# One square for both sums of a norm, and the second layer's memory products moved into latent attention

## The chip, the core and the metric

The kernel runs on one core of a Trainium2 chip. The metric is the device time of one execution in microseconds. All times below are of that core. "PE" is TensorE, "DVE" VectorE, "ACT" ScalarE, "POOL" GpSimd, "SP" the engine that issues most transfers; "PEld" is TensorE's load of the stationary operand, which overlaps its products.

## The reference

Two blocks run one after the other on a sequence of 512 rows of 1024 numbers. The first block ends in a mixture of experts and a norm with factor `final_norm_g`. The second block has two layers; each begins with a norm, so that at the seam two norms follow each other directly. Each layer computes three attentions (sliding window, sparse, latent), joins them, and then attends to a memory of 256 rows:

```python
def rmsnorm(x, g):
    x32 = x.astype(jnp.float32)
    y = x32 * lax.rsqrt(jnp.mean(x32 * x32, axis=-1, keepdims=True) + NORM_EPS)
    return (y * g.astype(jnp.float32)).astype(x.dtype)

for l in range(DEPTH_2):
    h = rmsnorm(x, norm_mix[l])
    ...                      # w_in, window, sparse and latent attention, w_out
    x = x + cross_attn(rmsnorm(x, norm_xattn[l]), rmsnorm(mem, norm_mem[l]),
                       w_xq[l], w_xkv[l], w_xo[l])
    ...                      # feed-forward
```

In `cross_attn` the memory side is `hm @ w_kv`, a 256 x 1024 by 1024 x 1024 product: columns 0 to 511 are the keys of four heads, 512 to 1023 their values. It depends on the inputs alone, not on x, so each layer's can be computed at any time before that layer's cross attention.

## The kernel before

Activations of block 2 lie transposed: eight tiles of 128 partitions (channels) by 512 columns (rows of the sequence), `xT[:, k]`. Most products are made in float32r with both operands split into a high and a low part (`hi_lo`, L36): three products for each chunk of 128 channels (`mmT`, L1173, lines L1179 to L1181), summed in a PSUM bank. `block128` (L1183) loads 128 columns of a weight, splits them (ACT high, DVE low) and makes the 24 products of eight chunks into a bank with tag "mm", of which there are two. Weights pass through three raw tiles (`wr`) and two split ones each (`wh`, `wl`).

The order of the work: the kernel is written as straight code, and a planner orders each engine's instructions by a simulated time, with earlier program text first. `self.fill` is a list of pieces of work; `pump` (L1000) takes some from it, and `share` (L1008) spreads the rest over the heads that are left, so that PE has something to do while a head's softmax runs on ACT and DVE.

`first_norm` (L1126) is the seam between the blocks. `norm_add` makes the high and low parts of x times both factors (`nh`, `nl`). For the sums it makes two squares for each chunk, of x (ACT and POOL in turn, L1139 and L1141) and of x times `final_norm_g` (ACT, L1142), and sums each over its 128 channels with a float32 product against 32 columns of ones (L1144), four chunks side by side in the four 32-row quarters of one bank, so two banks. Both are copied (L1146, L1147); eight float32 products with the column `pick` (L1151) add the four quarters and turn the sums into columns; a dozen small DVE steps make the two inverse roots, and `spread` (L132, product on L135, copy on L136) makes rows of them. The products of layer 0 don't wait for these rows: `scaled` (L1189) applies r to a bank behind the products. `layer` (L1382) begins with columns 512 (keys) and 640 (values) of `w_in_2` for the sliding window.

`mem_kv` (L1743) makes layer 1's memory products in eight parts of 128 columns behind a `start` that loads the normed memory `mh` (two halves, high and low, written to DRAM by `memory`, L1086, during block 1). Each part loads weights, splits them (L1760 on ACT, L1761 on POOL or DVE), makes 24 products of 256 columns, splits the result and stores it (L1774). Parts 4 to 7 also turn the result with two transposes (L1772). Parts 0 to 3 are put in at the end of `first_norm` (L1167), parts 4 to 7 before layer 0's cross attention (L1535), which takes them as fill (L1781, L1838). Layer 0's own memory products (`mem_kv0`, L1720) are made in block 1 in plain float32. The latent attention is the loop `self.heads(mla, oc)` (L1522) with the list of L1521 as fill.

Of the kernel before, what the change touches and what calls it, by code (L numbers as in the profile page):

```python
# [24 lines left out]
class Kern:  # L25
# [158 lines left out]
    def run(self):  # L184
        tc, nc, a = self.tc, self.nc, self.a
        with tc.tile_pool(name="cst", bufs=1, reuse_waits="tile") as self.cst, tc.tile_pool(name="dr0", bufs=1, space=bass.MemoryType.DRAM) as self.dram0, ExitStack() as self.late:
            cst = self.cst
            self.pst = "t"
            self.nraw, self.nw = 0, 0
            self.fill, self.side, self.kvd = [], [], [self.dram0.tile([8, P, 512], F32, name=f"kv{l}") for l in range(2)]  # L190
            self.xT = cst.tile([P, ND, T], F32, name="xT")
            self.ident = self.const("k_ident")
            self.ones = cst.tile([P, P], F32, name="ones")
            nc.vector.memset(self.ones, 1.0)
            self.pick = cst.tile([P, 1], F32, name="pick")
            nc.vector.reduce_sum(self.pick, self.ident[:, 0:P:32], axis=AX)
            self.block1()
            self.block2()
# [773 lines left out]
    def unit(self, name, dt=F32R):  # L972
        return self.sp.tile([P, 512], dt, tag="un", name=name, bufs=self.NU)
# [4 lines left out]
    def block2(self):  # L978
# [92 lines left out]
    def memory_rows(self):  # L1071

        nc = self.nc
        self.memd = self.dram0.tile([P, 2, 4, 512], F32, name="memd")
# [11 lines left out]
    def memory(self, tms, i):  # L1086
# [6 lines left out]
        m = [self.tmp("m", F32R) for _ in range(2)]  # L1093
        for s in range(2):
# [31 lines left out]
    def first_norm(self):  # L1126
# [22 lines left out]
        for i in range(2):  # L1149
            for t in range(NT):  # L1150
                nc.tensor.matmul(ps[:, 4 * i + t:4 * i + t + 1], rows[i][:, t * P:(t + 1) * P], self.pick, start=True, stop=True)  # L1151
        v = self.sp.tile([P, 8], F32, name="v8")
        nc.vector.tensor_scalar(v, ps[:, :8], 1.0 / D, None, op0=ALU.mult)
# [13 lines left out]
        self.fill += self.mem_kv(1, range(4), True)  # L1167
        self.pump(4)
# [213 lines left out]
    def layer(self, l, h, r, xd):  # L1382
# [7 lines left out]
        va = self.v_stack(self.scaled(self.block128(W, 640, h), r))  # L1390
# [130 lines left out]
        self.fill += [lambda: pair(1)] + b1[0:1] + [lambda: pair(2)] + b1[1:2] + [lambda: pair(3)] + b1[2:]  # L1521
# [12 lines left out]
        if l == 0:  # L1534
            self.fill += self.mem_kv(1, range(4, 8))  # L1535
# [207 lines left out]
    def mem_kv(self, l, parts, pool=False):  # L1743

        nc, a = self.nc, self.a
        W = a["w_xkv_2"][l]
        hm = ([], [])
        d = self.kvd[l]

        def start():  # L1750
            for i in range(4):
                for z in range(2):
                    m = self.unit("mh")
                    nc.sync.dma_start(m.bitcast(F32), self.memd[:, z, i])
                    hm[z].extend(m[:, 256 * s:256 * s + 256] for s in range(2))

        def part(i):
            raw = self.wraw(W, 0, ND, i * P, P)
            w = self.wtiles(ND, P)
            nc.scalar.copy(w[0], raw)  # L1760
# [4 lines left out]
            if i < 4:  # L1765
                self.hi_lo(ps[:, :256], t[:, 0:256], t[:, 256:512])
            else:
                f = self.tmp("xv")
                nc.scalar.copy(f[:, :256], ps[:, :256])
                pt = self.bank("pt", 2)  # L1770
                for q in range(2):
                    nc.tensor.transpose(pt[:, q * P:(q + 1) * P], f[:, q * P:(q + 1) * P], self.ident)  # L1772
                self.hi_lo(pt[:, :256], t[:, 0:256], t[:, 256:512])
            nc.sync.dma_start(d[i], t.bitcast(F32))  # L1774
# [212 lines left out]
```

## Time and profile before

| | |
|---|---|
| median of three runs | 3110.28 us (3108.94 to 3110.70) |
| profiled execution | 3112.91 us, its span 3111.1 us |
| PE busy | 2962.9 us (95%) |
| DVE, ACT, POOL busy | 1805.3, 1295.6, 170.6 us |
| mean granted TensorE clock | 0.983 |
| mean load of the DMA engines | 159 GB/s |

The span runs from the first to the last instruction; the execution has 1.8 us around it. The page cuts the span into 40 slices: PE is at 9 tenths or more in nearly all. Block 1 and the experts take the first 1006 us, layer 0 the time to about 2070, layer 1 the rest. Matmuls are pipelined, so their durations overlap; the step from one start to the next is what a product costs.

### The profile page before, as it was taken

The page shows a single profiled execution, that of the slowest core. Times are in us where ns is not written, and L with a number is a line of the kernel's source. Part 1 is how long each engine was busy: PE and PEld are TensorE (multiplying, and loading weights), DVE is VectorE, ACT ScalarE, POOL GpSimd, SP SyncE. Part 2 cuts the span into 40 slices and gives each one's busy share as a digit, 9 for nine tenths or more (in the row PEclk, how much of TensorE's full clock was granted, in tenths as well). Part 3 has the DMA queues.
Part 4 walks back from the last instruction along what each step waited for, and adds up shares of the span by engine and source line. Part 5 has one row for each costly group of instructions (what it writes and reads, how often), then busy time and mean ns, then how long its engine had stood idle before and what let it go on. Part 6 is the DMA issues. An engine that isn't in the chain of part 4 may idle for free.

```text
span 3111.1 us, 39214 instructions
## 1 busy us (share of the span) xinstructions
PE 2962.9 (95%) x14752; PEld 2237.4 (72%) x14752; DVE 1805.3 (58%) x3246; ACT 1295.6 (42%) x2482; POOL 170.6 (5%) x163
## 2 busy tenths in 40 slices
PE   7999999998987999999999999999999999999998
PEld 2887776443322788887878888878888887788886
DVE  7566774343334666567666553556766777655354
ACT  5333342322222444468645322233555775432233
POOL 1000211000000100000110000000000002000000
PEclk8998999999999999999999999999999999999999
DMA  7433677999999542223253333344322234233332
GB/s 256 123 99 101 195 228 276 384 409 409 409 409 367 147 114 73 73 85 104 79 167 111 102 89 101 90 118 115 89 70 78 83 93 132 91 109 90 102 94 81
DMA packets 478113, 493.57 MB, mean 159 GB/s; under 512 B 30182, under 2 KB 381668, under 8 KB 477924
## 3 DMA queue, kind: packets, MB, share of 16 engines
q1 hardware_dynamic: 474260, 481.05, 47.1%
q0 software_dynamic: 2224, 5.82, 0.6%
q10 hardware_dynamic: 1440, 4.19, 0.4%
q8 instruction: 116, 1.90, 0.3%
q14 instruction: 73, 0.60, 0.1%
HBM read 458.76 MB, written 32.24 MB: 158 GB/s over the span
## 4 chain that ended last, share of the span: by engine, by line
PE 59%; DVE 4%; ACT 3%; issue 1%; POOL 0%; ACTq 0%; DVEq 0%; POOLq 0%
PE mm L1179 11%; PE mm L1180 11%; PE mm L1181 11%; PE s L1181 3%; PE s L1180 3%; PE s L1179 3%; PE o L1179 3%; PE o L1180 3%; PE o L1181 3%; PE s L1274 2%; PE pt L1258 1%; PE o L1300 1%; DVE wl L40 1%; ACT p L1284 1%; ACT p L1277 1%
## 5 line engine op out<-in xcount | busy, mean ns | idle before, releaser
L39 ACT CAST wh<-wr 128x1024 fp32r<-128x1024 f32 (+6 forms) x433 | 377.1, 874 | 827.7 <-issue 264.6
L40 DVE TENSOR_TENSOR wl<-wr,wh 128x1024 fp32r<-128x1024 f32 (+7 forms) x431 | 459.2, 1068 | 232.1 <-ACT wh L39 230.2
L1179 PE MATMUL mm<-nh,wh 128*128 128x512 f32 x1136 | 449.7, 396 | 9.4 <-DVE gt L1541 4.4
L1181 PE MATMUL mm<-nh,wl 128*128 128x512 f32 x1136 | 447.3, 394 | 0.1
L1180 PE MATMUL mm<-nl,wh 128*128 128x512 f32 x1136 | 446.1, 393 | 0.0
L1179 PEld LDWEIGHTS mm<-nh,wh 128*128 128x128 f32 x1136 | 214.2, 189 | 56.2 <-DVE gt L1541 7.3
L1181 PEld LDWEIGHTS mm<-nh,wl 128*128 128x128 f32 x1136 | 214.3, 189 | 44.4 <-issue 0.8
L1180 PEld LDWEIGHTS mm<-nl,wh 128*128 128x128 f32 x1136 | 214.2, 189 | 43.7 <-issue 1.2
L1181 PE MATMUL o<-ah,wl 128*128 128x512 f32 x352 | 137.5, 391 | 0.0
L1180 PE MATMUL s<-nl,wh 128*128 128x512 f32 x352 | 137.2, 390 | 0.0
L1179 PE MATMUL o<-ah,wh 128*128 128x512 f32 x352 | 137.2, 390 | 0.0
L1179 PE MATMUL s<-nh,wh 128*128 128x512 f32 x352 | 137.2, 390 | 0.0
L1180 PE MATMUL o<-al,wh 128*128 128x512 f32 x352 | 137.0, 389 | 0.0
L1181 PE MATMUL s<-nh,wl 128*128 128x512 f32 x352 | 137.0, 389 | 0.0
L40 DVE TENSOR_TENSOR pl<-pt,ph 128x512 fp32r<-128x512 f32 (+1 forms) x192 | 115.7, 606 | 31.7 <-ACT ph L39 30.5
L857 PE MATMUL u<-pc,xg 128*64 128x512 f32 x512 | 121.5, 601 | 12.5 <-DMA pc<-in_w_up_e 11.0
L857 PE MATMUL g<-pc,xg 128*64 128x512 f32 x512 | 120.7, 600 | 6.4 <-DMA pc<-in_w_gate_e 3.5
L1277 ACT ACTIVATE p<-s,nm 128x128 f32<-128x128 f32 x192 | 101.5, 531 | 52.7 <-DVE nm L1276 45.7
L39 ACT CAST ph<-pt 128x512 fp32r<-128x512 f32 (+1 forms) x192 | 99.3, 524 | 52.1 <-PE pt L1258 47.9
L1276 DVE TENSOR_REDUCE nm<-s 128x1 f32<-128x128 f32 x192 | 92.1, 484 | 49.3 <-PE s L1275 48.1
L76 PE MATMUL mm<-hx,wh 128*128 128x512 f32 (+1 forms) x296 | 120.5, 407 | 0.0
L78 PE MATMUL mm<-hx,wl 128*128 128x512 f32 (+1 forms) x296 | 118.9, 402 | 0.5 <-DVE wl L40 0.5
(644 smaller groups left out, 6088.7 us busy)
## 6 DMA issues: line engine op xcount, KB each, us to landing
pc<-in_w_gate_e SPq DMA_DIRECT2D x64, 1024.0 KB
pc<-in_w_up_e SPq DMA_DIRECT2D x64, 1024.0 KB
wr<-in_w_in SPq DMA_DIRECT2D x122, 512.0 KB
pc<-in_w_down_e SPq DMA_DIRECT2D x60, 1024.0 KB
wr<-in_w_gate_up SPq DMA_DIRECT2D x88, 512.0 KB
aw<-in_ada_w SPq DMA_DIRECT2D x40, 512.0 KB
wr<-in_w_out SPq DMA_DIRECT2D x24, 512.0 KB
gd<-gt SPq DMA_DIRECT2D x32, 256.0 KB
```

Of the source, the lines that this page charges most:

```text
L39: nc.scalar.copy(hi, src)
L40: nc.vector.tensor_tensor(lo, src, hi.bitcast(F32), op=ALU.subtract)
L76: nc.tensor.matmul(ps, w[0](kw), x[0](kx), start=start and i == 0, stop=False)
L78: nc.tensor.matmul(ps, w[1](kw), x[0](kx), start=False, stop=stop and i == n - 1)
L857: nc.tensor.matmul(pss[h][64 * side:64 * side + 64, :], x[:, c, :], w[:, k, h * 512:(h + 1) * 512], start=c < 2, stop=c > 5)
L1179: nc.tensor.matmul(ps, wh, x[0][k], start=start and i == 0, stop=False)
L1180: nc.tensor.matmul(ps, wh, x[1][k], start=False, stop=False)
L1181: nc.tensor.matmul(ps, wl, x[0][k], start=False, stop=stop and i == n - 1)
L1258: nc.tensor.transpose(pt[:, i * P:(i + 1) * P], b, self.ident)
L1274: nc.tensor.matmul(s[:, :N], q[:, t * P:(t + 1) * P], k[:, :N], start=i == 0, stop=False)
L1276: nc.vector.tensor_reduce(nm[:, t:t + 1], s[:, :N], op=ALU.max, axis=AX, negate=True)
L1277: nc.scalar.activation(p[t][:, :N], s[:, :N], AF.Exp, bias=nm[:, t:t + 1], accum_out=den[:, t:t + 1])
```

## The change

In the first norm one square of x for each chunk, all on ACT, and a stationary operand `gsq[:, k]` of 32 columns: 16 of ones and 16 of the squared factor. One product then gives both sums, 16 rows each, in one bank. `pick` gets two columns, and four products in place of eight make both columns. `gsq` is made on POOL at the start of block 2, and the four loads of the rope tables move from ACT's queue to POOL's. The products of columns 640 are held behind the last column product in layer 0 (`issue_after`). Unit tiles (tag "un") get a pool of their own, which lies behind the others.

The memory of layer 1 is stored as one float32 half (`memory` writes one tile, not two). Its products become plain float32 with no split: parts 0 to 3 eight products of 256 columns, parts 4 to 7 sixteen of 128 with the memory as the stationary operand, so that no transposes are needed. Parts 0 to 3 become the last fill of layer 0's latent attention, parts 4 to 7 that of layer 1's.

```diff
-            self.pick = cst.tile([P, 1], F32, name="pick")
-            nc.vector.reduce_sum(self.pick, self.ident[:, 0:P:32], axis=AX)
+            self.pick = cst.tile([P, 2], F32, name="pick")
+            for i in range(2):
+                nc.vector.reduce_sum(self.pick[:, i:i + 1], self.ident[:, 16 * i:P:32], axis=AX)
...
     def unit(self, name, dt=F32R):
-        return self.sp.tile([P, 512], dt, tag="un", name=name, bufs=self.NU)
+        return self.up.tile([P, 512], dt, tag="un", name=name, bufs=self.NU)
...
+            tc.tile_pool(name="un", bufs=1, reuse_waits="tile") as self.up,
...
+            self.gsq = self.cst.tile([P, ND, 32], F32, name="gsq")
+            nc.gpsimd.memset(self.gsq, 1.0)
+            gf = self.c1["final_norm_g"].unsqueeze(2).to_broadcast([P, ND, 16])
+            nc.gpsimd.tensor_tensor(self.gsq[:, :, 16:32], gf, gf, op=ALU.mult)
...
-                nc.scalar.dma_start(t, self.roped[i])
+                nc.gpsimd.dma_start(t, self.roped[i])
...
-            self.hi_lo(ps[:, c], *(h[:, c] for h in m), scale=g1[:, k:k + 1])
-        for z in range(2):
-            nc.sync.dma_start(self.memd[:, z, i], m[z].bitcast(F32))
+            nc.scalar.activation(m[:, c], ps[:, c], AF.Copy, scale=g1[:, k:k + 1])
+        nc.sync.dma_start(self.memd[:, i], m)
...
-        psr = [self.bank("o", 2) for _ in range(2)]
+        psr = self.bank("o", 2)
         for k in range(ND):
-            q = slice(32 * (k % 4), 32 * (k % 4) + 32)
-            sq, sg = (self.unit(s, F32) for s in ("sq", "sg"))
-            if k % 2:
-                nc.scalar.activation(sq, xT[:, k], AF.Square)
-            else:
-                nc.gpsimd.tensor_tensor(sq, xT[:, k], xT[:, k], op=ALU.mult)
-            nc.scalar.activation(sg, xT[:, k], AF.Square, scale=gf[:, k:k + 1])
-            for ps, s in zip(psr, (sq, sg)):
-                nc.tensor.matmul(ps[q, :], self.ones[:, 0:32], s, start=k < 4, stop=k > 3)
-        rows = [self.tmp("row") for _ in range(2)]
-        nc.scalar.copy(rows[0], psr[0])
-        nc.vector.tensor_copy(rows[1], psr[1])
+            q, sq = 32 * (k % 4), self.unit("sq", F32)
+            nc.scalar.activation(sq, xT[:, k], AF.Square)
+            nc.tensor.matmul(psr[q:q + 32, :], self.gsq[:, k, :], sq, start=k < 4, stop=k > 3)
+        row = self.tmp("row")
+        nc.scalar.copy(row, psr)
...
-                nc.tensor.matmul(ps[:, 4 * i + t:4 * i + t + 1], rows[i][:, t * P:(t + 1) * P], self.pick, start=True, stop=True)
+            self.mark = nc.tensor.matmul(ps[:, 2 * t:2 * t + 2], row[:, t * P:(t + 1) * P], self.pick, start=True, stop=True).ins
...
-        self.fill += self.mem_kv(1, range(4), True)
-        self.pump(4)
...
-        va = self.v_stack(self.scaled(self.block128(W, 640, h), r))
+        with self.tc.issue_after(self.mark) if l == 0 else ExitStack():
+            ps = self.block128(W, 640, h)
+        va = self.v_stack(self.scaled(ps, r))
...
-        self.fill += [lambda: pair(1)] + b1[0:1] + [lambda: pair(2)] + b1[1:2] + [lambda: pair(3)] + b1[2:]
+        self.fill += [lambda: pair(1)] + b1[0:1] + [lambda: pair(2)] + b1[1:2] + [lambda: pair(3)] + b1[2:] + self.mem_kv1(range(4 * l, 4 * l + 4))
...
-        if l == 0:
-            self.fill += self.mem_kv(1, range(4, 8))
...
+    def mem_kv1(self, parts):
+        nc, W, hm = self.nc, self.a["w_xkv_2"][1], []
         def start():
             for i in range(4):
-                for z in range(2):
-                    m = self.unit("mh")
-                    nc.sync.dma_start(m.bitcast(F32), self.memd[:, z, i])
-                    hm[z].extend(m[:, 256 * s:256 * s + 256] for s in range(2))
+                m = self.unit("mh", F32)
+                nc.sync.dma_start(m, self.memd[:, i])
+                hm.extend(m[:, 256 * s:256 * s + 256] for s in range(2))
         def part(i):
             raw = self.wraw(W, 0, ND, i * P, P)
-            w = self.wtiles(ND, P)
-            nc.scalar.copy(w[0], raw)
-            (nc.gpsimd if pool else nc.vector).tensor_tensor(w[1], raw, w[0].bitcast(F32), op=ALU.subtract)
             ps = self.bank("mm", 2)
-            self.mmT(ps[:, :256], w, 0, P, hm, range(ND))
+            for q in range(1 if i < 4 else 2):
+                for k in range(ND):
+                    o, lhs, rhs = (ps[:, :256], raw[:, k], hm[k]) if i < 4 else (ps[:, q * P:q * P + P], hm[k][:, q * P:q * P + P], raw[:, k])
+                    nc.tensor.matmul(o, lhs, rhs, start=k == 0, stop=k == ND - 1)
             t = self.sp.tile([P, 512], F32R, tag="gt", name="xkv", bufs=3)
...
+            self.hi_lo(ps[:, :256], t[:, 0:256], t[:, 256:512])
+            nc.sync.dma_start(self.kvd[1][i], t.bitcast(F32))
```

## Rows read from the trace of the kernel before

**Rows 1.** The page, part 1: busy us, share of the span, instructions.
```profile
PE 2962.9 (95%) x14752; PEld 2237.4 (72%) x14752; DVE 1805.3 (58%) x3246; ACT 1295.6 (42%) x2482; POOL 170.6 (5%) x163
```

**Rows 2.** PE in order of time: start, us, line, product [idle before <- releaser].
```profile
1006.05 0.39 PE L942 MATMUL u<-ohT,y 128*128 128x512 f32 x1
1011.75 2.56 PE L1144 MATMUL o<-sq,ones 128*32 128x512 f32 x4 [5.31 <-POOL sq L1141]
...
1034.11 0.50 PE L1179 MATMUL mm<-nh,wh 128*128 128x512 f32 x1
...
1047.39 0.39 PE L1181 MATMUL mm<-nh,wl 128*128 128x512 f32 x1
```

**Rows 3.** Busy time by stretch: length, PE, PEld, DVE, ACT, POOL, granted clock, DMA, GB/s.
```profile
1010.00:1020.00 10.00, 8.25 (x30) 3.24 (x34) 8.57 (x9) 8.19 (x14) 6.03 (x9) 0.69 0.90 295
...
1480.00:1490.00 10.00, 10.00 (x44) 9.52 (x44) 4.46 (x11) 4.01 (x13) 0.00 (x0) 0.52 0.01 2
```

**Rows 4.** The chain of waits from 1009 to 1031: start, us, what.
```profile
1011.75 4.26 PE o L1144 x8
...
1016.52 1.83 PE o L1144 x6
...
1019.74 1.85 PE o L1144 x12
...
1022.26 0.97 PE o L1144 x2
...
1028.99 1.68 PE pt L1151 x16
```

**Rows 5.** PE alone in a stretch of memory products: length, PE, clock, DMA, GB/s.
```profile
1030.50:1034.00 3.50, 3.50 (x31) 1.00 0.61 170
```

**Rows 6.** Instructions of lines L43 (seam, next norm) and L1141: ns min/median/max.
```profile
L43 DVE SCALAR_TENSOR_TENSOR nl<-xT,g,nh x8: 737/1130/1522, 1010.1 to 1017.8; 128x512 fp32r<-128x512 f32 x8
...
L43 DVE SCALAR_TENSOR_TENSOR nl<-xT,cols,nh x8: 746/746/749, 1593.7 to 1628.7; 128x512 fp32r<-128x512 f32 x8
...
L1141 POOL TENSOR_TENSOR sq<-xT x4: 1277/1482/1484, 1010.4 to 1014.5; 128x512 f32<-128x512 f32 x4
```

**Rows 7.** DVE and ACT in order of time, around the norm's factors.
```profile
1030.71 0.17 DVE L1153 TENSOR_SCALAR v<-pt 128x8 f32<-128x8 f32 x1 [1.54 <-PE pt L1151]
...
1040.77 0.59 ACT L136 COPY rstd<-pt 128x512 f32<-128x512 f32 x1
```

**Rows 8.** A group of POOL's loads (busy us, mean ns), and a stretch of block 1.
```profile
L696 POOL DMA_DIRECT2D u<-ud x4 | 2.1, 536 | 0.3 <-DVE pmn L708 0.3
...
444.00:454.00 10.00, 10.00 (x47) 6.62 (x45) 9.21 (x17) 5.60 (x11) 0.00 (x0) 1.00 0.45 130
```

**Rows 9.** PE in order of time at the ends of both cross attentions; memory products by stretch.
```profile
1626.22 0.39 PE L1181 MATMUL mm<-yh,wl 128*128 128x512 f32 x1
...
1710.48 0.39 PE L1181 MATMUL s<-xoh,wl 128*128 128x512 f32 x1
...
2663.04 0.39 PE L1181 MATMUL mm<-yh,wl 128*128 128x512 f32 x1
...
2731.54 0.39 PE L1181 MATMUL s<-xoh,wl 128*128 128x512 f32 x1
...
1626.60:1710.90 84.30, 15.46 (x96) 14.62 (x96) 0.00 (x0) 0.00 (x0) 0.96 0.41 131
```

**Rows 10.** Float32 products: PE in order of time in block 1, chain of waits at the seam.
```profile
496.48 12.68 PE L1730 MATMUL mm<-pre,hm 128*128 128x256 f32 x58
...
1039.84 1.78 PE pt L135 x16
```

**Rows 11.** Latent attention of layer 0: two stretches, and PE's longest wait (us, times, longest).
```profile
1540.00:1550.00 10.00, 10.00 (x64) 8.95 (x63) 5.81 (x13) 7.51 (x18) 1.28 (x1) 1.00 0.30 83
1560.00:1570.00 10.00, 8.15 (x27) 5.87 (x28) 7.27 (x10) 3.97 (x7) 3.37 (x2) 0.83 0.35 106
...
PE mm L1179 <- ACT oh L39: 2.0, 1, 2.0
```

More of the change, by code (lines that the diff above doesn't have):

```diff
@@ L1073, in memory_rows @@
         nc = self.nc
-        self.memd = self.dram0.tile([P, 2, 4, 512], F32, name="memd")
+        self.memd = self.dram0.tile([P, 4, 512], F32, name="memd")
         two = lambda k: self.xT[:, k:k + 2].rearrange("p a c -> p (a c)")
@@ L1092, in memory @@
         ps = self.bank("t", 2)
-        m = [self.tmp("m", F32R) for _ in range(2)]
+        m = self.tmp("m")
         for s in range(2):
@@ L1132, in first_norm @@
             self.norm_add(n, k, xT[:, k], False)
-        psr = [self.bank("o", 2) for _ in range(2)]
+        psr = self.bank("o", 2)
         for k in range(ND):
-            q = slice(32 * (k % 4), 32 * (k % 4) + 32)
-            sq, sg = (self.unit(s, F32) for s in ("sq", "sg"))
-            if k % 2:
-                nc.scalar.activation(sq, xT[:, k], AF.Square)
-            else:
-                nc.gpsimd.tensor_tensor(sq, xT[:, k], xT[:, k], op=ALU.mult)
-            nc.scalar.activation(sg, xT[:, k], AF.Square, scale=gf[:, k:k + 1])
-            for ps, s in zip(psr, (sq, sg)):
-                nc.tensor.matmul(ps[q, :], self.ones[:, 0:32], s, start=k < 4, stop=k > 3)
-        rows = [self.tmp("row") for _ in range(2)]
-        nc.scalar.copy(rows[0], psr[0])
-        nc.vector.tensor_copy(rows[1], psr[1])
+            q, sq = 32 * (k % 4), self.unit("sq", F32)
[3 more added lines that the diff above has]
+        nc.scalar.copy(row, psr)
         ps = self.bank("pt", 2)
-        for i in range(2):
-            for t in range(NT):
-                nc.tensor.matmul(ps[:, 4 * i + t:4 * i + t + 1], rows[i][:, t * P:(t + 1) * P], self.pick, start=True, stop=True)
+        for t in range(NT):
+            self.mark = nc.tensor.matmul(ps[:, 2 * t:2 * t + 2], row[:, t * P:(t + 1) * P], self.pick, start=True, stop=True).ins
         v = self.sp.tile([P, 8], F32, name="v8")
-        nc.vector.tensor_scalar(v, ps[:, :8], 1.0 / D, None, op0=ALU.mult)
+        nc.vector.tensor_scalar(v.rearrange("p (j t) -> p t j", j=2), ps[:, :8].rearrange("p (t j) -> p t j", j=2),
+                                1.0 / D, None, op0=ALU.mult)
         nc.vector.tensor_scalar(v[:, 0:4], v[:, 0:4], EPS, None, op0=ALU.add)
@@ L1741, in mem_kv0 @@
         nc.gpsimd.dma_start(self.kvd[0][2 * i:2 * i + 2].rearrange("s p c -> p s c"), w[:, 2:6].rearrange("p (s z) c -> p s (z c)", z=2))
[L1743 to L1748, printed above, removed]
+    def mem_kv1(self, parts):
+        nc, W, hm = self.nc, self.a["w_xkv_2"][1], []
         def start():
             for i in range(4):
-                for z in range(2):
-                    m = self.unit("mh")
-                    nc.sync.dma_start(m.bitcast(F32), self.memd[:, z, i])
-                    hm[z].extend(m[:, 256 * s:256 * s + 256] for s in range(2))
+                m = self.unit("mh", F32)
+                nc.sync.dma_start(m, self.memd[:, i])
+                hm.extend(m[:, 256 * s:256 * s + 256] for s in range(2))
         def part(i):
             raw = self.wraw(W, 0, ND, i * P, P)
-            w = self.wtiles(ND, P)
-            nc.scalar.copy(w[0], raw)
-            (nc.gpsimd if pool else nc.vector).tensor_tensor(w[1], raw, w[0].bitcast(F32), op=ALU.subtract)
             ps = self.bank("mm", 2)
-            self.mmT(ps[:, :256], w, 0, P, hm, range(ND))
+            for q in range(1 if i < 4 else 2):
+                for k in range(ND):
+                    o, lhs, rhs = (ps[:, :256], raw[:, k], hm[k]) if i < 4 else (ps[:, q * P:q * P + P], hm[k][:, q * P:q * P + P], raw[:, k])
+                    nc.tensor.matmul(o, lhs, rhs, start=k == 0, stop=k == ND - 1)
             t = self.sp.tile([P, 512], F32R, tag="gt", name="xkv", bufs=3)
[L1765 to L1774, printed above, removed]
+            self.hi_lo(ps[:, :256], t[:, 0:256], t[:, 256:512])
+            nc.sync.dma_start(self.kvd[1][i], t.bitcast(F32))
         return [start] + [lambda i=i: part(i) for i in parts]
```

## The prediction, made before the changed kernel was timed

> **What bounds the kernel now.** The page comes first: TensorE (PE) is busy 95% of the span, VectorE (DVE) 58%, ScalarE (ACT) 42%, GpSimd (POOL) 5% [rows 1]. So time is won where PE waits or runs on its half clock, or where it has less to do; the change touches three such places, and each is read by itself.
>
> The first is the seam between the mixture of experts and the first norm of block 2. PE's order of time [rows 2] shows the last scatter product at 1006.05 us, then 5.3 us with nothing until the first row sum (L1144), which waits for a square made on POOL. The first product of layer 0 (columns 512 of `w_in_2`) starts at 1034.11, and the second block (columns 640) ends at 1047.39. Those 41 us hold 48 wide products of layer 0, worth 11.5 us (the last 13.3 us less the 1.78 us of L135 between the blocks [rows 10]), and much else. The granted clock is 0.69 in the slice after the wait [rows 3]: part of it on 1.2 instead of 2.4 GHz. The chain of waits [rows 4] says what else: 32 row-sum instructions in six stretches, 4.26, 1.83, 1.85 and three of 0.97 us, 10.9 us together; narrow products of the memory between them; 16 instructions of L1151 in 1.68 us. The second place is the cross attention of layer 0, which has four memory parts as fill; that of layer 1 has none. The third is the latent attention, where the change puts all eight parts.
>
> **The change part by part. Seam, PE.** Three of the four parts planned here run before 1034. One part is 24 products (three float32r products for each of eight chunks). In the stretch 1030.5 to 1034.0 there are 31 instructions in 3.5 us at full clock [rows 5], 30 gaps, so 0.117 us each: 72 x 0.117 = 8.4 us leave the seam. The fourth part runs later, in the sliding-window attention, where PE is full: 24 x 0.117 = 2.8 us. The row sums halve, from 32 instructions to 16 (one square per chunk in place of two): 10.9 / 2 = 5.4 us. L1151 goes from 16 to 8: 1.68 / 2 = 0.8 us. Together 8.4 + 5.4 + 0.8 = 14.6 us.
>
> What the 16 remaining row sums cost depends on how the planner groups them. Twelve together took 1.85 us, a pair alone between full-width products 0.97 us [rows 4]: 16 cost between 2.5 (16 x 0.154) and 7.8 us (8 x 0.97). I take 5.4, half of what there is, since the planner has again full-width products, those of block 512, to put between them. The Trainium skill, "TensorEngine Tiling (Array Packing)", section Tiling Modes, states that a switch of the tiling mode drains the engine, which speaks against such a mixture. By that rule with a switch at each pair the row sums would cost 7.8 us and the whole sum below would lose 2.4 us; the pairs agree with the rule, the stretch of twelve shows that no switch need come.
>
> **Seam, waits.** With the first weights of layer 0 in the queue instead of the memory's, PE can run block 512 in the 5.3 us wait, one chunk behind ACT and DVE. DVE gets faster as well: its eight low parts there took 0.74 to 1.52 us each while POOL squared beside them, and 0.75 in the next norm of layer 0, where POOL is idle [rows 6]; 8 squares on ACT replace 12 on ACT and 4 on POOL. I count 4 us of the 5.3 as filled; bounds are 0 and 5.3 + 3.1, the last being the half clock of rows 3 (10 x 0.31), which goes too if PE never stops. A new wait stands against this: block 640 is held behind the last column product (`issue_after`), which needs ScalarE's copy of the sums; its 24 products and all that is planned after them on PE queue there. Block 512 covers it, unless it is already done: 1.5 us, bounded by 0 and the 5.5 us of block 640. Then 14.6 + 4 - 1.5 = **17.1 us** won at the seam, bounds 7 and 26.
>
> After block 640 both "mm" banks wait for the norm's r. Before, the first DVE step of v starts at 1030.71 and ScalarE copies r at 1040.77 [rows 7], but between them DVE also splits weights and the results of memory parts, and the spread (L135) stands behind block 512 on PE. I take r as ready when block 640 ends; the other case is a rival.
>
> Steps moved here that I cost at nothing: four rope loads go from ACT's queue to POOL's (0.54 us an issue for another load there [rows 8], 2.2 us in all) with the fill and square of `gsq` ahead of them (under 2 us by POOL's 1.43 us for a four times larger square [rows 6]). POOL loses 4 squares and 4 splits there, so it has room; the first row sum waits for `gsq`, and if the cover is gone that costs up to 2 us. ACT gets its queue back ahead of the first `nh`. Eight 256 KB loads of `mh` leave SP's queue. The `un` tiles lie elsewhere, so the first `nh` may start earlier or later; the trace shows no addresses, and the bounds of the 5.3 us wait take this in. In block 1 eight low parts of DVE and four stores go; PE is busy 10.00 of 10.00 us there [rows 8], so nothing.
>
> **Cross attention of layer 0.** Here the trace holds its own experiment. From the last output product to the last product of `w_xo` layer 0 needs 1710.48 - 1626.22 = 84.26 us, with 96 memory products; layer 1, with the same attention and no fill, 2731.54 - 2663.04 = 68.50 us [rows 9]. So the fill costs **15.8 us** and goes. The bare products would be 96 x 0.117 = 11.2 us, the lower bound; the rest are waits and half clock (0.96 granted in that stretch).
>
> **Latent attention, both layers.** Each part becomes plain float32. Layer 0's kind (weights first, 256 columns) is 8 products, 16 instructions; the same product for layer 0's own memory in block 1 shows 58 instructions in 12.68 us [rows 10], 0.219 each: 3.5 us a part, 14.0 for four. Layer 1's kind is 32 instructions of 128 columns; 16 float32 products of 128 columns took 1.78 us [rows 10], 0.111 each: 3.56 a part, 14.2 for four. Is PE full there? In slices near its end it is 10.00 of 10.00 and then 8.15 [rows 11]; the one long wait is 2.0 us for the last head (`oh`), with clock 0.83 behind it, in each layer. So little hides the parts: I take 1 us a layer as filled (bounds 0 and 4, the wait and its clock). 14.0 + 14.2 - 2 = **26.2 us** more. DVE and ACT add 8 pairs of 0.4 us steps and lose the splits of the weights. SP carries 4 loads, 4 weights and 4 stores a layer; a store waits for its low part with the next weights behind it, as it did in the cross attention.
>
> **Sum.** -17.1 - 2.8 - 15.8 + 26.2 = -9.5 us. Against the profiled run's 3112.91 us that is 3103.4; that run is 2.6 us over the median of the three, 3110.28, against which I forecast **3100.8 us**. The likeliest case's own range is 3095 to 3106.
>
> **The rivals.**
> (A) Larger gain: `nh` starts during the last scatter, so PE runs through the seam at full clock (all 5.3 + 3.1 us), the row sums go in one group (2.5 us, 2.9 less), no new wait; and the parts fill the 2.0 us wait in each latent attention and save its clock (4 a layer). -25.9 - 2.8 - 15.8 + 20.2 = -24.3: 3086 us. For it: a wait that depends on POOL is gone. Against it: the parts stand ahead of the last head in program order, so they are likely spent before that wait.
> (B) r is late: if it needs the same 10 us from the column products as in rows 7, it comes some 4.7 us after block 640, with both banks full: 3105.5 us. For it: DVE still has the splits of two or three weight tiles to do in that stretch.
> (C) Slower: the parts block the softmax in latent attention. Each holds an "mm" bank, a raw weight slot and PE's in-order queue for 3.5 us, and heads and branches behind it start late. The savings elsewhere are 35.7 us; from 35.7 / 8 = 4.5 us a part the kernel is slower, and one half-clock stretch like 1480 to 1490 (0.52 granted [rows 3], 4.8 us lost) in each layer adds 1.2 a part. With that and 0.7 us of late weights a part costs 5.4: 43.2 - 35.7 = 7.5 us over, 3118 us. For it: such a stretch stands in this very attention. Against it: the longest wait of PE there is 2.0 us [rows 11].
>
> **How the numbers follow.** Chances: the forecast 0.55, A 0.20, B 0.16, C 0.09. A change within 0.2% (6.2 us, up to 3104.1 or 3116.5) can hardly be told from none. The forecast's case lies below 3104.1 four times in five (0.44), A always, B one time in four (0.04): faster 0.68; same 0.23; slower 0.09. The range for 8 in 10 runs from A's 3086 to 3109, beyond B, leaving out C and the far end of A.
>
> **What would show it.** After the change: no `mh` rows before 1400 us; the first `nh` product before 1016 instead of 1034; block 640's end 17 us nearer to the last scatter product; the cross attention of layer 0 at 68 to 69 us; the latent stretches 12 to 14 us longer each with float32 rows of 0.22 and 0.11 us. It would be wrong if r stands out as a PE wait after block 640, if the cross attention does not shorten to layer 1's, or if the latent stretches grow by over 18 us.

## The result

The changed kernel took 3155.23 us (median of four runs, 3152.37 to 3157.19) against 3109.94 us for the kernel before: 1.0143 times as long, 95% interval 1.0129 to 1.0157. The forecast was 3100.8 us, with 3086 to 3109 as its range and a chance of 0.09 for slower. Its profiled execution has a span of 3153.1 us, 42.0 more than before.

Line numbers of the changed kernel: the products of `mmT` are L1177 to L1179, the row sums L1145, the column products L1150, the memory products L1757. First its page, part 1, which answers to [rows 1]:

```profile
PE 3006.6 (95%) x14720; PEld 2241.5 (71%) x14720; DVE 1793.0 (57%) x3234; ACT 1283.0 (41%) x2466; POOL 159.6 (5%) x161
```

PE has 32 instructions fewer and is busy 43.7 us longer. PEld, DVE, ACT and POOL hardly differ. So the time is not in a new wait; products have become dearer.

PE's order of time at the seam, which answers to [rows 2] (start, duration, line, tiles, count, idle time ahead of it):

```profile
1009.09 0.63 PE L943 MATMUL sc<-ohT,y 128*128 128x512 f32 x1
1009.52 0.63 PE L943 MATMUL u<-ohT,y 128*128 128x512 f32 x1
1009.94 0.63 PE L1177 MATMUL mm<-nh,wh 128*128 128x512 f32 x1
1013.48 0.50 PE L1178 MATMUL mm<-nl,wh 128*128 128x512 f32 x1 [2.91 <-DVE nl L43]
...
1017.69 0.40 PE L1177 MATMUL mm<-nh,wh 128*128 128x512 f32 x1
1018.02 1.04 PE L1145 MATMUL o<-sq,gsq 128*32 128x512 f32 x2
1019.00 0.50 PE L1178 MATMUL mm<-nl,wh 128*128 128x512 f32 x1
1019.34 0.40 PE L1179 MATMUL mm<-nh,wl 128*128 128x512 f32 x1
...
1023.63 1.05 PE L1145 MATMUL o<-sq,gsq 128*32 128x512 f32 x4
...
1025.28 1.06 PE L1145 MATMUL o<-sq,gsq 128*32 128x512 f32 x6
1027.08 1.05 PE L1150 MATMUL pt<-pick,row 128*128 128x2 f32 x8 [0.75 <-ACT row L1147]
1027.99 0.48 PE L1177 MATMUL mm<-nh,wh 128*128 128x512 f32 x1
...
1033.44 0.40 PE L1179 MATMUL mm<-nh,wl 128*128 128x512 f32 x1
1033.67 1.95 PE L135 MATMUL pt<-k_ident,rs 128*128 128x128 f32 x16
1036.13 0.50 PE L1177 MATMUL mm<-nh,wh 128*128 128x512 f32 x1 [0.51 <-DVE sc L1189]
...
1043.93 0.63 PE L1234 MATMUL pt<-k_ident,sc 128*128 128x128 f32 x4 [1.47 <-DVE sc L1189]
1044.31 0.48 PE L1572 MATMUL mm<-nh,wh 128*128 128x512 f32 x1
```

The first `nh` product starts 0.4 us behind the last scatter product, where 28 us lay between them before [rows 2]. The last scatter products start 0.43 us apart at a granted clock of 0.50 (1007.4 to 1010.0 us), and before 0.23 us apart at 1.00; that is part of the later end of the scatter here. Block 640 runs from 1027.99 to 1033.67, behind the column products as the change wants it, and its last product starts 23.9 us after the last scatter product instead of 41.3. The stretches that answer to [rows 3] and to the half clock in the latent attention (columns: stretch, length, busy time of PE, PEld, DVE, ACT, POOL, granted clock, share of the DMA engines, GB/s):

```profile
1010.00:1020.00 10.00, 7.09 (x20) 4.04 (x19) 8.06 (x12) 7.71 (x14) 0.00 (x0) 0.81 0.37 75
1489.00:1499.00 10.00, 9.04 (x40) 8.29 (x41) 5.30 (x12) 6.58 (x17) 0.00 (x0) 0.66 0.25 73
```

And the memory's products by tile (durations min/median/max in ns, first and last start). They stand in the latent attention of each layer and nowhere else:

```profile
L1757 PE MATMUL mm<-wr,mh x128: 272/275/325, 2596.9 to 2616.6; 128*128 128x128 f32 x128
L1757 PE MATMUL mm<-mh,wr x64: 377/379/430, 1536.5 to 1555.0; 128*128 128x256 f32 x64
```

Where the 42 us lie can be read from the start times of the same instructions in the traces. Three bounds are steps of DVE: the first gate's product times r, the last addition behind `w_out` in layer 0, and the last up product of layer 0's feed-forward times r (what is left of that feed-forward counts to the next row). The others are first or last products on PE. The last column is a run told below, in which only the place of the unit tiles differs from the changed kernel:

| stretch, us | before | after | after, unit tiles 32 bytes on |
|---|---|---|---|
| start to last scatter product | 1006.1 | 1009.5 | 1007.3 |
| to the first gate | 60.9 | 45.5 | 47.2 |
| to latent attention, layer 0 | 391.5 | 396.9 | 392.2 |
| latent attention, layer 0 | 123.7 | 139.3 | 140.1 |
| output product `w_out`, layer 0 | 44.4 | 45.6 | 44.5 |
| cross attention, layer 0 | 83.8 | 68.6 | 66.2 |
| feed-forward, layer 0, to its last up product | 312.4 | 321.4 | 312.4 |
| to latent attention, layer 1 | 476.2 | 483.8 | 474.8 |
| latent attention, layer 1 | 120.0 | 140.3 | 139.6 |
| `w_out` and cross attention, layer 1 | 112.5 | 112.7 | 110.7 |
| rest | 379.6 | 389.4 | 379.8 |

The seam and the cross attention gained, the latent attention lost more than was forecast, and then there are some 33 us in stretches that the change does not touch: 9.0 in layer 0's feed-forward, 9.8 in the rest behind layer 1's cross attention, 7.6 ahead of layer 1's latent attention. One window inside the feed-forward shows what these have in common. Here PE never waits and the clock is full in both kernels, so the count of instructions is the price of one. Before:

```profile
1760.00:2000.00 240.00, 240.00 (x1061) 1.00 0.33 98
```

After (here and in the other windows of this stretch: length, PE busy and count, granted clock, DMA share, GB/s):

```profile
1760.00:2000.00 240.00, 240.00 (x1030) 1.00 0.32 95
```

240 / 1061 is 226.2 ns a product, 240 / 1030 is 233.0: the same products, on a full clock, 6.8 ns dearer. In block 1, whose tiles the change does not move, the step is 227 ns in both traces. The memory's plain float32 products, which read unit tiles too, have the same step in the changed kernel and in the runs below that move the unit tiles: 216 ns with 256 columns and 112 with 128 (medians).

### The profile page after: what moved, and what is told of

The parts are those of the page before. It is cut to its first block, busy times and chain, and to the rows that moved or that the text cites. A ratio compares the mean times of both kernels' runs of the same rounds, so it can differ in the third digit from the quotient of the medians.

```text
span 3153.1 us, 39079 instructions
## 1 busy us (share of the span) xinstructions
PE 3006.6 (95%) x14720; PEld 2241.5 (71%) x14720; DVE 1793.0 (57%) x3234; ACT 1283.0 (41%) x2466; POOL 159.6 (5%) x161
## 4 chain that ended last, share of the span: by engine, by line
PE 80%; DMA 7%; DVE 7%; ACT 4%; issue 2%; POOL 0%; SPq 0%; ACTq 0%; DVEq 0%; POOLq 0%
PE mm L1177 11%; PE mm L1178 11%; PE mm L1179 11%; PE s L1179 3%; PE s L1178 3%; PE s L1177 3%; PE o L1179 3%; PE o L1177 3%; PE o L1178 3%; PE u L858 2%; PE g L858 2%; PE mm L78 2%; PE mm L76 2%; PE mm L77 2%; DMA pc<-in_w_down_e 2%; DMA pc<-in_w_up_e 2%
## 5 line engine op out<-in xcount | busy, mean ns | idle before, releaser
L40 DVE TENSOR_TENSOR wl<-wr,wh 128x1024 fp32r<-128x1024 f32 (+7 forms) x431 | 456.3, 1061 | 240.8 <-ACT wh L39 239.1
L1177 PE MATMUL mm<-nh,wh 128*128 128x512 f32 x1136 | 456.9, 402 | 11.3 <-DVE sc L1189 6.3
L1178 PE MATMUL mm<-nl,wh 128*128 128x512 f32 x1136 | 452.9, 399 | 2.9 <-DVE nl L43 2.9
L1179 PE MATMUL mm<-nh,wl 128*128 128x512 f32 x1136 | 454.2, 400 | 0.0
L1177 PEld LDWEIGHTS mm<-nh,wh 128*128 128x128 f32 x1136 | 215.3, 189 | 63.3 <-DVE sc L1189 7.7
L1179 PEld LDWEIGHTS mm<-nh,wl 128*128 128x128 f32 x1136 | 215.0, 189 | 50.3 <-issue 1.7
L1179 PE MATMUL o<-ah,wl 128*128 128x512 f32 x352 | 139.6, 397 | 0.0
L1177 PE MATMUL s<-nh,wh 128*128 128x512 f32 x352 | 139.4, 396 | 0.0
L1177 PE MATMUL o<-ah,wh 128*128 128x512 f32 x352 | 139.4, 396 | 0.0
L1179 PE MATMUL s<-nh,wl 128*128 128x512 f32 x352 | 139.2, 395 | 0.0
L858 PE MATMUL u<-pc,xg 128*64 128x512 f32 x512 | 123.8, 601 | 13.2 <-DMA pc<-in_w_up_e 11.7
```

The source lines that it names most:

```text
L40: nc.vector.tensor_tensor(lo, src, hi.bitcast(F32), op=ALU.subtract)
L858: nc.tensor.matmul(pss[h][64 * side:64 * side + 64, :], x[:, c, :], w[:, k, h * 512:(h + 1) * 512], start=c < 2, stop=c > 5)
L1177: nc.tensor.matmul(ps, wh, x[0][k], start=start and i == 0, stop=False)
L1178: nc.tensor.matmul(ps, wh, x[1][k], start=False, stop=False)
L1179: nc.tensor.matmul(ps, wl, x[0][k], start=False, stop=stop and i == n - 1)
```

## The experiments

**Address or work.** Theory one: the price is the address. The diff gives the unit tiles, which are the moving operand of most products of block 2, a pool of their own. The addresses that the allocator gave in the two kernels (a trace has none) are 73504 + 2048 i before and 137216 + 2048 i after; the split weights `wh` and `wl` lie at 46880 + 4096 i in both. By 64, the weights leave a remainder of 32, the unit tiles 32 before and 0 after. Rivals: the region of the buffer, and the memory parts or another piece of the work. Four kernels tell these apart.

The changed kernel with 32 unused bytes ahead of the unit tiles:

```diff
             self.wps = [self.wp]
+            self.up.tile([P, 8], F32, name="pad")
```

> The changed kernel with one unused tile of 32 bytes allocated ahead of the unit tiles in their new pool: every unit tile lies 32 bytes higher, so its address modulo 64 is 32 again, as in the kernel before; all the work stays. Theory (address phase): in the changed kernel a 128x512 product whose moving operand is a unit tile starts 233.3 ns after the one ahead of it, before 227; some 6,400 of them make 42 us. With the phase back the step is 227 ns and the time 3155.2 - 42 = 3113 us (3105 to 3118). Rival one (the region of the buffer that the tiles lie in, not the phase): step 233, 3155 us. Rival two (the memory parts block the softmax, or any other piece of the work itself): 3155 us.

3121.64 us (seven runs), 1.0033 of the kernel before (1.0022 to 1.0044): 33.6 us come back for 32 bytes. That is less than the 42 put down, and the time lies above the range of theory one, but the step is the one that it named. The feed-forward window:

```profile
1760.00:2000.00 240.00, 240.00 (x1061) 1.00 0.33 95
```

The kernel before with the same shift (the tiles behind the unit tiles in their pool move along):

```diff
         n = self.norm_start(self.g12)
+        self.sp.tile([P, 8], F32, name="pad")
         for k in range(ND):
             self.norm_add(n, k, xT[:, k], False)
+        self.sp.tile([P, 8], F32, name="pad")
```

> The kernel before with an unused tile of 32 bytes ahead of the unit tiles in their pool and a second one behind them: the unit tiles and the small-stage tiles behind them lie 32 and 64 bytes higher than before in the same region, with the unit tiles at addresses that are multiples of 64 as in the changed kernel; all the work is that of the kernel before. Theory (address phase): step of the products from unit tiles 227 to 233 ns, time 3110 + 42 = 3152 us (3145 to 3158). Rival one (region): 3110 us. Rival two (the new work): 3110 us.

3147.16 us, 1.0114 (1.0099 to 1.0129): 37 us slower with none of the change's work, in the old region of the buffer. The same window:

```profile
1760.00:2000.00 240.00, 240.00 (x1030) 1.00 0.32 94
```

So it is neither the work nor the region. Weights and unit tiles together 32 bytes up:

```diff
             nc.vector.memset(self.ones, 1.0)
+            cst.tile([P, 8], F32, name="pad")
```

> The changed kernel with an unused tile of 32 bytes in the pool of constants that lies below everything: weights, tables, and unit tiles all move 32 bytes up. The unit tiles lie at 32 modulo 64, the weight tiles (32 before) at 0, and in the first block moving operand and weights both at 0. It tells what the phase is counted against. If the moving tile's own address decides: second block's step 227, first block's 227 to 233 (some 960 wide products there, +6 us), about 3119 us. If the distance of moving tile to weight tile decides: second block stays at 233, first block stays at 227, 3155 us. If neither (the work): 3155 us with the steps as they are.

3153.0 us, 1.0138 (1.0121 to 1.0155). The unit tiles lie where they are cheap in the first run, and they are dear; the products of block 1, both of whose operands moved, stay at 227 ns. So not the moving tile's own address decides but how it stands to the weight tile. The window:

```profile
1760.00:2000.00 240.00, 240.00 (x1030) 1.00 0.32 93
```

Unit tiles back in the old pool, all else as changed:

```diff
-        return self.up.tile([P, 512], dt, tag="un", name=name, bufs=self.NU)
+        return self.sp.tile([P, 512], dt, tag="un", name=name, bufs=self.NU)
```

> The changed kernel with the unit tiles back in the pool of the other second-block tiles, as in the kernel before: they start at 74528 instead of 137216, with 32 modulo 64, so region and phase are both nearly those of the kernel before; the rest of the change stays. Theory (addresses, by phase or by region): step 227, about 3113 us (3105 to 3118). Against the run with the shifted pool it tells whether the region matters beside the phase. Rival (the new work itself): 3155 us.

3118.64 us (ten runs), 1.0025 (1.0016 to 1.0035), 36.6 us below the changed kernel. Theory one stands here too, though the time is 0.6 us above its range. This is the change with its tiles in the right phase, and it is still slower than the kernel before where a gain of 9.5 us had been forecast.

**How the two have to agree.** Two more kernels complete the picture: everything 32 bytes up and the unit tiles another 32 (both pads above), and the changed kernel with 96 bytes ahead of the unit tiles (`[P, 24]` in the first pad).

> The changed kernel with everything moved 32 bytes up and the unit tiles another 32: weight tiles and unit tiles both at 0 modulo 64. It completes the square of phases (weights 32 with units 0: 3155 us; 32 with 32: 3122; 0 with 32: 3153). If the step depends on whether the two agree modulo 64: 227 ns, 3120 us. If the unit tiles have to lie at 32, or the weights have to: 233 ns, 3155 us.

3123.95 us, 1.0033 (1.0019 to 1.0046), with this window:

```profile
1760.00:2000.00 240.00, 240.00 (x1060) 1.00 0.33 96
```

> The changed kernel with 96 unused bytes ahead of the unit tiles instead of 32: unit tiles and weights agree modulo 64 but differ by 64 modulo 128 (with 32 bytes they agreed modulo 128 as well). If only the remainder by 64 counts: step 227 ns, 3121 us. If the remainder by 128 counts: step 233 ns or another, 3150 to 3158 us.

3128.38 us, 1.0062 (1.0046 to 1.0078), with this window:

```profile
1760.00:2000.00 240.00, 240.00 (x1050) 1.00 0.33 97
```

| weights, remainder by 128 | unit tiles, by 128 | step in the window, ns |
|---|---|---|
| 32 (before) | 32 | 226.2 |
| 32 (after) | 0 | 233.0 |
| 32 (32 bytes) | 32 | 226.2 |
| 64 (everything moved) | 32 | 233.0 |
| 64 (both moved) | 64 | 226.4 |
| 32 (96 bytes) | 96 | 228.6 |

The second run of the first group, with 32 and 64, had 233.0 as well. Where the two agree by 128 the step is 226; where they differ by 32, to either side, it is 233; where they agree by 64 alone it is 228.6 in the mean, between the two values put down, so a third of the loss (2.4 of 6.8 ns) comes back when 128 is missed. This mean hides three values. By the starts in this window, 226 ns follow on `nh` times `wh`, 229 on `nl` times `wh` and 232 on `nh` times `wl`, chunk by chunk; in the changed kernel 233 to 234 ns follow on each of the three. Why the engine minds, the runs do not say.

**The rest of the miss.** In the right phase the kernel is 8.7 us (unit tiles back in the pool) or 11.7 us (32 bytes) above the kernel before, not 9.5 below. The two halves of the change were run alone, both with unit tiles in the old phase. The seam alone:

```diff
-            for ps, s in zip(psr, (sq, sg)):
-                nc.tensor.matmul(ps[q, :], self.ones[:, 0:32], s, start=k < 4, stop=k > 3)
+            nc.tensor.matmul(psr[q:q + 32, :], self.gsq[:, k, :], sq, start=k < 4, stop=k > 3)
...
+        with self.tc.issue_after(self.mark) if l == 0 else ExitStack():
+            ps = self.block128(W, 640, h)
```

> The kernel before with the seam's part of the change alone: one square per chunk, row sums over columns of ones and squared factors, block 640 held behind the column products. The memory parts stay float32r and stand where they stood (four at the seam, four in the cross attention of layer 0), rope loads on ScalarE's queue, unit tiles in the phase of the kernel before (32 modulo 64). By the terms of the prediction (row sums 5.4, columns 0.8, filled wait 4, new wait -1.5) it gains 8.7 us: 3110 - 8.7 = 3101 us. Rival one (the memory parts at the seam are now in the way, since they take the wait that the new order fills): half of it, 3105 us. Rival two (the new row sums give nothing, r comes no earlier): 3110 us.

3112.31 us (eleven runs, 3108.13 to 3119.21), 1.0007 (0.9998 to 1.0016): no difference, where 8.7 us were forecast. From the last scatter product to the first gate its trace has 59.7 us, the kernel before 60.9. PE's waits at the seam of this run (line, tile, releaser: total, times, longest):

```profile
PE o L1143 <- ACT sq L1142: 5.0, 1, 5.0
PE x L943 <- ACT y L934: 2.6, 1, 2.6
PE mm L1177 <- DVE xkv L40: 1.2, 1, 1.2
PE mm L1179 <- POOL wl L1761: 1.2, 1, 1.2
```

The 5.3 us wait of [rows 2] is still there, released by ACT instead of POOL, and behind it PE's queue has the memory's products and not yet block 512, which was to fill it. Two new waits of 1.2 us hang on the memory's own splits (L1761 on POOL, the result `xkv` on DVE). So the shorter sums brought PE sooner to work whose operands were not ready. The memory alone:

```diff
-        self.fill += self.mem_kv(1, range(4), True)
-        self.pump(4)
...
-        self.fill += [lambda: pair(1)] + b1[0:1] + [lambda: pair(2)] + b1[1:2] + [lambda: pair(3)] + b1[2:]
+        self.fill += [lambda: pair(1)] + b1[0:1] + [lambda: pair(2)] + b1[1:2] + [lambda: pair(3)] + b1[2:] + self.mem_kv1(range(4 * l, 4 * l + 4))
```

> The kernel before with the memory's part of the change alone: all eight parts in plain float32, four in the latent attention of each layer, none at the seam or in the cross attention; the old two row sums; unit tiles in the old phase. By the terms of the prediction (parts out of the seam -8.4 and -2.8, cross attention -15.8, latent attention +26.2) it is 0.8 us faster: 3109 us. Rival (the latent attention pays all of its parts and their waits: it grew by 16.9 and 14.5 us in the run with unit tiles back in their pool, and the fourth part gave no 2.8 us): 3110 - 8.4 - 15.9 + 31.4 = 3117 us; then the two halves add up to the 3118.6 us of that run with a seam that gives nothing more.

3121.6 us, 1.0036 (1.0023 to 1.0048): 10.4 us slower against 0.8 faster by the forecast's terms, and 4.6 us above the rival as well. The seam on top of it gives 3.0 us (the 3118.64 us of the fourth run), which the two intervals don't separate. So both halves miss their forecast, the seam by some 10 us and the memory by 11. In the memory's trace the stretch to the first gate gains 7.7 us where 11.2 were forecast, the two latent attentions grow by 16.3 and 13.4 us, 29.7 in place of 26.2, and the stretch ahead of layer 1's grows by 2.1. The last product for the scatter came 1.9 us later than before; in all eleven kernels with the memory stored once it came at 1007.3 to 1011.0 us, in the three others at 1004.3 to 1006.5. In the expert stage ahead of it PE waits for its weight loads (the DMA engines move 400 to 409 GB/s from 610 to 980 us in both traces); why the scatter ends later is not settled.

What the parts cost in the latent attention by themselves was asked of a kernel that makes one chunk of products in place of eight in each part:

```diff
-                for k in range(ND):
+                for k in range(1):
```

> The run with the unit tiles back in their pool (3118.6 us), with one of the eight chunks of each memory part's products left out of nothing else: seven eighths of the products of parts 0 to 7 are not computed (24.6 of 28.1 us of PE time), loads, evictions and stores stay. It prices the products in the latent attention by themselves. By the prediction's terms (2 us of 28.2 hidden) the time falls by 23 us to 3095.6. If PE is not the limit everywhere there, it falls by less, 15 us (3103). If the products also cause waits and half clock, it falls by more than 24.6 us, 3090.

3089.55 us, 29.1 less than the 3118.64 us of the same kernel with all products: more than the 24.6 us that they take, as in the third case put down. The latent attention of both layers with all products, and then with an eighth of them (columns as in the first windows):

```profile
1446.00:1587.00 141.00, 132.36 (x731) 113.06 (x730) 90.84 (x164) 84.73 (x201) 23.78 (x15) 0.95 0.38 112
2489.00:2624.00 135.00, 128.10 (x799) 111.67 (x798) 90.49 (x166) 84.37 (x200) 23.11 (x15) 0.99 0.40 118
```

```profile
1446.00:1573.00 127.00, 119.99 (x680) 103.40 (x679) 91.62 (x167) 83.83 (x200) 23.58 (x15) 0.95 0.43 125
2475.00:2597.00 122.00, 114.69 (x686) 99.12 (x686) 89.47 (x164) 83.22 (x200) 23.16 (x15) 0.99 0.43 126
```

The stretches shorten by 14 and 13 us, PE's busy time by 12.4 and 13.4. PE is idle 8.6 and 6.9 us with the parts and 7.0 and 7.3 without: the fill fills nothing there. The waits and the half clock that the third case named do not show, since idle time and granted clock hardly differ; the products cost their own time and a little more. The longest wait of PE in layer 0's stretch, for the last head (`oh`), is 2.1 us in both.

Two more pieces were moved. The rope loads back on ACT's queue:

```diff
-                nc.gpsimd.dma_start(t, self.roped[i])
+                nc.scalar.dma_start(t, self.roped[i])
```

> The run with the unit tiles back in their pool (3118.6 us, everything else of the change in it), and the four rope loads back on ScalarE's queue instead of GpSimd's. Theory (the loads on GpSimd's queue wait there for the expert stage's buffers and hold up what GpSimd issues behind them; the last scatter product came 2.0 us later than before): the scatter ends near 1006, 3116.5 us. Rival (the queue does not matter): 3118.6 us, scatter's end at 1008.

3122.05 us, 1.0034 (1.0022 to 1.0046), with the last scatter product at 1011.0: the theory falls. The queue is not what makes the scatter late; whether POOL's is better by 3 us can't be told, since the intervals overlap. And parts 4 to 7 in the cross attention of layer 0, as float32:

```diff
+        if l == 0:
+            self.fill += self.mem_kv1(range(4, 8))
         h, r = self.cross(l, h, r)
```

> The run with the unit tiles back in their pool (3118.6 us), with the float32 parts 4 to 7 as fill in the cross attention of layer 0, where the kernel before had them, instead of the latent attention of layer 1. In layer 1 the latent attention should lose its 14.5 us; the cross attention of layer 0, at 68.4 us without parts, grows. Theory (the cross attention has waits that the fill covers: there 11.2 us of products cost 15.8 before with their splits and transposes, which float32 does not have): 14.3 us of products cost 10 there, 3114 us. Rival (a part costs the same wherever PE is full): 3118.6 us.

3126.86 us, 1.0047 (1.0034 to 1.0059): against both expectations it is dearer. In its trace layer 1's latent attention loses 10.4 us, and layer 0's cross attention grows from 68.0 to 85.2 us, past the 83.8 us that it took with the float32r parts. Float32 saves the splits there and makes the products longer (14.3 us against 11.2).

**A better place.** The three placements cost as much as the products or more, and the seam's own run shows 5 us in which PE has nothing that is ready. Plain float32 parts need only loads. So parts 0 to 3 go ahead of the first norm, 4 to 7 into the cross attention, all else as in the run with the unit tiles back:

```diff
+            self.fill += self.mem_kv1(range(4))
+            self.pump(5)
             h, r, xd = self.first_norm()
```

> The run with the unit tiles back in their pool (3118.6 us), with the float32 memory parts 0 to 3 ahead of the first norm instead of the latent attention of layer 0, and 4 to 7 in the cross attention of layer 0. A float32 part needs no split of its weights, so PE can run it while ScalarE and VectorE make the first norm's tiles (5 us without PE work there in the run with the seam alone). Theory: of 13.8 us of products 5 to 8 stand in that wait and keep the clock up; against the kernel before the seam gains 3 to 6 us and the cross attention loses 1: 3106 us. Rival (weights and memory rows land too late for the wait, PE's queue stands behind them): 3113 us or more.

3106.15 us (eleven runs), 0.9987 of the kernel before (0.9978 to 0.9996): the one kernel with all of the work that is below the kernel before, by 0.13%. PE's order of time at its seam:

```profile
1008.75 0.40 PE L943 MATMUL u<-ohT,y 128*128 128x512 f32 x1
1011.28 8.86 PE L1760 MATMUL mm<-mh,wr 128*128 128x256 f32 x32 [2.13 <-DVE xT L945]
1020.07 1.92 PE L1146 MATMUL o<-sq,gsq 128*32 128x512 f32 x16
1021.92 7.17 PE L1760 MATMUL mm<-mh,wr 128*128 128x256 f32 x32
1028.93 0.95 PE L1151 MATMUL pt<-pick,row 128*128 128x2 f32 x8
```

Two parts run while ACT and DVE make the first norm's tiles, and two while ACT copies the sums. From the last scatter product to the first gate it is 50.7 us, with 46.7 in the run that has no parts there: four parts for 4.0 us, where the latent attention of layer 0 took 16.9 for them (140.6 against 123.7 us before). And all sixteen row sums stand together, in 1.92 us, where pairs between full-width products take 1.04 each. The time put down was met in part by luck: against the kernel before the seam gains 10.2 us, not 3 to 6, but the scatter ends 2.7 us later, and the latent attention of layer 0 is 3.9 us shorter and that of layer 1 4.2 longer, neither of which had been forecast.

## Why the prediction was wrong, step by step

- **The unit tiles' pool** is the step that failed. The prediction said that they "lie elsewhere, so the first `nh` may start earlier or later", and let the bounds of the 5.3 us wait take it in. It looked for what a new place does to waits and not to the products that read it. It cost 33.6 us in the changed kernel and 37.2 alone in the kernel before: 62% of the 54.4 us between forecast and result. No rival had it: rival C, the one on the slower side, has another mechanism, the softmax blocked, and PE's longest wait in the changed kernel's latent attention of layer 0 is 2.1 us, against 2.0 before. Of the other 20.8 us the trace of the run with 32 bytes shows 13.1 (latent attention 9.8 over the forecast, seam 6.2, scatter 1.2; cross attention 1.8 and the other stretches 2.3 under it); the rest is how far the two profiled executions lie from the medians of their kernels.
- **The seam** was right up to the point that was named and wrong behind it. Forecast: block 640's end 17 us nearer to the last scatter product; measured 41.3 to 23.9, 17.4 nearer. The row sums went as said (16 in pairs of 1.04 us and two longer groups, 5.0 us by their starts, 5.4 forecast). But of the 5.3 us wait 2.91 stayed, now on DVE's `nl` (4 forecast as filled, 2.4 measured), and "I take r as ready when block 640 ends" failed: L135 (1.95 us) stood ahead of block 640 and now stands behind it, with waits of 0.51 and 1.47 us that before had products under them. That is part of rival B (2.5 us of its 4.7 up to the next block). From the last scatter product to the first gate the seam and the fourth part gain 15.4 us in the changed kernel and 13.7 with 32 bytes, 19.9 forecast.
- **The price of a group of row sums** was read wrongly, though the sum came out near. The prediction weighed the rule of the Trainium skill, "TensorEngine Tiling (Array Packing)", section Tiling Modes, that a switch of the mode drains the engine, and took the price of a pair as a sign of it. But in the changed kernel four instructions and six (1.05 and 1.06 us) take no longer than two (1.04): by the starts in the trace the two instructions of one quarter follow each other by 0.45 us, those of different quarters start together, and the sixteen of the last run start four at a time. So a pair is dear in the main because it has one quarter to itself. No run shows the price of a switch apart. What is left for it is some 0.3 us a group: 0.33 us from the product ahead to the group and 0.34 from the first product behind it to the next, in place of 0.23, and 0.53 us behind the second instruction in place of 0.45.
- **The sum of independent terms** failed for the seam as well: with the memory in place its sums are worth nothing measurable (1.0007), forecast 8.7 us. The term "wait filled 4" depended on the other half of the change.
- **The cross attention**: 15.8 forecast from layer 1's own stretch [rows 9], 15.2 measured, 17.6 with 32 bytes. The one term that rested on a whole stretch of the trace without the work held.
- **The latent attention**: 26.2 forecast; 16.4 and 19.6 us, 36.0, in the run with 32 bytes, and 16.9 and 14.5, 31.4, in the run with the unit tiles back, where layer 1's first product of that stretch comes 3.5 us later behind the stretch ahead. The product prices were right (steps of 216 and 112 ns against 0.219 and 0.111 us). "1 us a layer as filled" was not: nothing was filled, and 24.6 us of products cost 27.4 in the two stretches and 29.1 in the medians. The bound below should have been the products' full time and the bound above should have lain beyond it; the forecast's own criterion, growth by over 18 us, is met in layer 1 with 32 bytes and not with the tiles back in their pool.
- **Moved at no cost**: the memory stored once in block 1 goes with a scatter that ends 1.2 to 4.9 us later in eleven kernels, against nothing forecast. The kernels differ in more than this, and by which way it acts is open.
- The sum against one profiled execution has an uncertainty that the forecast left out: the runs of one kernel differ by up to 11 us (3108.1 to 3119.2 with the seam alone, at mean clocks of 0.983 to 0.980), and the spans of the kernel before and of the first run above differ by 3.7 us, their medians by 11.7.

## What to carry to other kernels

A diff that moves a tile to another address is a change to every product that reads it: count those products, and for products like these keep the addresses of the moving operand and of the stationary one equal by 128 bytes. A few bytes of padding make it a cheap experiment, and a window in which PE is full on a full clock shows it as a count of instructions. Work called fill costs its price less the idle time that it demonstrably stands in; put it where the trace shows a wait and where its own operands are ready before that wait begins.

## What the runs showed of the hardware

A float32r product of 512 columns starts 226 ns after the one ahead of it when its moving and its stationary tile leave the same remainder by 128, 229 ns in the mean when they agree by 64 alone (226, 229 and 232 in turn), and 233 ns when they differ by 32, at a granted clock of 1.00 in each window and in either region of the buffer. That is 3% of each such product, and 29 to 37 us of the whole in four pairs of kernels (changed and shifted by 32, changed and back in the old pool, before and shifted, everything moved and both moved). No weight load's own duration shows it (median 187 or 188 ns in the window of the kernels before and changed); it is in the step. Plain float32 products that read the same unit tiles (medians of 216 ns with 256 columns, 112 with 128) show no such difference.
